# Hybrid streaming encoder on one core: norms ahead of the first products, block sums regrouped, first splits on GpSimd, scan steps ahead of weight steps

## The chip, the cores and the metric

The kernel runs on one core of a Trainium2 chip. The core has a matrix engine (TensorE, PE in the rows, with weight loads as PEld), a vector engine (VectorE, DVE), a scalar engine (ScalarE, ACT), GpSimd (POOL) and SyncE (SP), which here issues most DMA transfers. Each engine works through its own list of instructions in order; semaphores make one wait for another. SBUF is the on-chip memory of 128 partitions, PSUM the banks into which PE accumulates. The metric is the device time of one execution in microseconds (us); a kernel's time is the median of its runs. The profile comes from one more execution.

## The reference

One block over 1040 tokens (16 learned tokens and 1024 of the input), 1024 wide, all float32:

```
h = concat(meta_tokens, x)
u = rmsnorm(h) * norm_mix_g
proj = u @ w_in                     # mLSTM q,k,v,o,i,f and retention q,k,v,g: 4 + 4 heads
h_ml = sigmoid(o) * head_norm(mlstm_chunkwise(silu(conv4(q,k)), v, gates))
h_rt = silu(g) * head_norm(retention_chunkwise(rotary(q), rotary(k), v))
h = h + concat(h_ml, h_rt) @ w_out
a = causal_dwconv(rmsnorm(h) @ w_up)            # FF = 2816
h = h + (silu(a) * (rmsnorm(h) @ w_gate)) @ w_down
out = rmsnorm(h)[meta:]
```

Both chunked scans carry a state C from chunk to chunk: `num = scores @ v + q @ C`, then `C = decay * C + k^T v`. The head norm takes mean and variance of each token's 256 values.

## The kernel before

**Products.** Every large float32 product is made of three faster ones: each operand is split into hi (a rounded copy, made by ACT) and lo (the remainder, made by DVE), and hi·hi, hi·lo and lo·hi are accumulated in PSUM. On top of this most products are done in a scheme of seven block products instead of eight: the activations are cut into blocks 11, 12, 21, 22 (half of the tokens by half of the channels), and sums S1 to S4 of blocks (`usum`, split by `usplit`) are formed on DVE; the weights get such sums too.

**Opening.** The 1040 tokens come in five pieces (`RNG`). `first_norm(r)` squares a piece, adds the squares up, lets PE sum over partitions (pca), takes the square root and its reciprocal (rcola), has PE broadcast the result (pra), scales the piece in place (L652) and splits it into u11h/u11l and so on. Head 4 (the first of retention) is done in plain three-part form: `v4_group(c)` gives v and the gates of one chunk with the weights w0raw, split into w0hi/w0lo by `v0_split`, and `q4_group` gives q and k. Then come the block sums, and `o_steps(4)`, the first seven-block product (po4x, po4y), which uses S1 to S4 in its third to sixth product; `qk_steps(0)` (pq0x, pq0y) follows.

**Mixing heads.** From here the program deals steps out by a planner. `go(steps)` walks the products of a head's q/k, v and o weights; around each, `slot` runs one step (`tick`) of each pending generator (`pend`) and starts tasks from the list `side`: the scan steps of another head (`scan_a`: scores s, pt, kw; `scan_b`: u, n, C, the statistics bn), and what follows a scan. How many tasks start in a slot depends on an estimated load of DVE and ACT against PE (`load`, `RATE`, `watch`). Weight units are generators as well: `quartered` (splits and block sums of one weight), `m_unit`, `w_unit` (sums of w_out for later), `first_right`. They wait with `jwait` for raw weight tiles, of which there are four, and `m_unit` and `w_unit` also wait while `busy()` says that DVE or ACT is ahead of PE by more than 0.5. While this part is built, `pinned` keeps each engine's instructions in the order in which they were written; elsewhere a scheduler orders them.

**End of the mixer.** The product with w_out is the class `Seven` (object `mixw`), in stages 1, 65, 73, 4, 2 (pwx, pwy). Its first stage is dealt among the scan steps of head 7. In stages 65 and 73 DVE forms the right operands (wr, rr; `rsplit`, L1030), sums for later stages (`tsum`, L1098) and, at L1755, four sums for the last two tokens (acc<-wm,mm,acc), whose factors stand in the small table mm.

## Time and profile before

| | |
|---|---|
| median of 3 runs | 1598.24 us (1595.65 to 1604.74) |
| profiled execution | 1605.5 us, of which the span (first to last instruction) is 1603.7 us |
| mean granted PE clock | 0.974 of full speed |
| PE busy | 1511.2 us, 94% |
| DVE busy | 1112.6 us, 69% |
| ACT busy | 778.6 us, 49% |
| POOL busy | 67.5 us, 4% |

Rows of stretches read: start and end, length, then busy time and count for PE, PEld, DVE, ACT and POOL, the granted PE clock, the DMA share and GB/s. Rows of a timeline read: start, duration, engine, line, operation, output<-inputs, shape; in brackets the idle time of that engine just before, and what ended it. A row with xN at its end is N instructions in a row. Rows of waits read: who waited for what: us in total, times, the longest. The opening ends at about 118 us, where the first product of head 0 starts; the scans and weight products of the mixer go on to 800; the feed-forward part takes the rest.

### The profile page before, as it was taken

How to read it: one execution, taken by the hardware profiler on the slowest of the kernel's cores; microseconds unless marked ns; L12 is line 12 of the kernel's file. 1: busy time of each engine (PE TensorE's matmuls, PEld its weight loads, DVE VectorE, ACT ScalarE, POOL GpSimd, SP SyncE). 2: the span in 40 equal slices, each digit the busy share in tenths (PEclk: the TensorE clock that was granted, in tenths of full speed). 3: DMA queues.
4: the chain of work that ended last, by engine and by line, in shares of the span. 5: the costliest groups of instructions: out<-in, count | busy, mean ns of one | idle time of the engine just before them, and what ended most of it. 6: DMA issues, size and time to landing. Idle time of an engine off the chain costs nothing.

```text
span 1603.7 us, 25323 instructions
## 1 busy us (share of the span) xinstructions
PE 1511.2 (94%) x9799; PEld 1368.9 (85%) x9799; DVE 1112.6 (69%) x2161; ACT 778.6 (49%) x1506; POOL 67.5 (4%) x104
## 2 busy tenths in 40 slices
PE   5989998899899999899799999999999999999997
PEld 4878898799888989897588898999999999888887
DVE  6586666675686757683876678777766666677657
ACT  5244557574654355554345546544444444344444
POOL 0000000000000000000000000222220000000000
PEclk9899999999999999999899999999999999999999
DMA  6031235542654245659634225788874222943213
GB/s 221 27 106 55 73 119 172 164 121 78 152 180 155 80 119 170 185 173 371 219 104 132 86 82 182 206 204 205 210 188 113 79 79 81 372 164 112 92 53 106
DMA packets 107176, 232.17 MB, mean 145 GB/s; under 512 B 10808, under 2 KB 34048, under 8 KB 106880
## 3 DMA queue, kind: packets, MB, share of 16 engines
q1 hardware_dynamic: 96736, 201.12, 38.0%
q0 software_dynamic: 10176, 29.37, 9.6%
q8 instruction: 77, 1.26, 0.3%
q14 instruction: 43, 0.35, 0.1%
q10 hardware_dynamic: 144, 0.07, 0.0%
HBM read 179.10 MB, written 74.49 MB: 158 GB/s over the span
## 4 chain that ended last, share of the span: by engine, by line
PE 71%; DMA 12%; DVE 9%; issue 4%; ACT 4%; SPq 0%; POOL 0%; DVEq 0%; POOLq 0%; ACTq 0%
DMA accd<-raw_m 3%; PE pdx L671 3%; PE pdx L672 3%; PE pdx L673 3%; PE pup_x L672 2%; PE pup_x L673 2%; PE pga_x L672 2%; PE pup_x L671 2%; PE pga_x L673 2%; PE pga_x L671 2%; PE pdy L672 2%; PE pdy L671 2%; PE pdy L673 2%; PE pwx L672 2%; PE pwx L671 2%
## 5 line engine op out<-in xcount | busy, mean ns | idle before, releaser
L575 ACT CAST hi_up<-raw_up 128x512 fp32r<-128x512 f32 (+1 forms) x52 | 36.4, 719 | 106.0 <-PE pga_z L672 61.2
L671 PE MATMUL pup_x<-uh_g,hi_up 128*128 128x256 f32 (+1 forms) x240 | 67.1, 282 | 1.2 <-ACT uh_g L1612 1.2
L576 DVE TENSOR_TENSOR lo_ga<-fraw_ga,hi_ga 128x512 fp32r<-128x512 f32 (+1 forms) x52 | 41.9, 809 | 37.8 <-ACT hi_ga L575 37.6
L672 PE MATMUL pup_x<-ul_g,hi_up 128*128 128x256 f32 (+1 forms) x240 | 67.1, 281 | 0.1
L673 PE MATMUL pup_x<-uh_g,lo_up 128*128 128x256 f32 (+1 forms) x240 | 66.4, 282 | 0.0
L576 DVE TENSOR_TENSOR lo_up<-raw_up,hi_up 128x512 fp32r<-128x512 f32 (+1 forms) x52 | 41.3, 810 | 36.0 <-ACT hi_up L575 35.1
L576 DVE TENSOR_TENSOR lo_d<-rd,hi_d 128x1024 fp32r<-128x1024 f32 (+1 forms) x34 | 37.7, 1113 | 32.9 <-ACT hi_d L575 32.8
L575 ACT CAST hi_ga<-fraw_ga 128x512 fp32r<-128x512 f32 (+1 forms) x52 | 36.4, 719 | 45.6 <-PE pup_z L672 24.0
L672 PE MATMUL pdx<-ul_d,hi_d 128*128 128x512 f32 (+1 forms) x156 | 58.1, 375 | 0.0
L673 PE MATMUL pdx<-uh_d,lo_d 128*128 128x512 f32 (+1 forms) x156 | 57.6, 373 | 0.0
L575 ACT CAST hi_d<-rd 128x1024 fp32r<-128x1024 f32 (+1 forms) x34 | 32.3, 960 | 48.9 <-PE pdy L672 32.6
L672 PE MATMUL pdy<-ul_d,hi_d 128*128 128x512 f32 x132 | 51.9, 393 | 0.0
L673 PE MATMUL pdy<-uh_d,lo_d 128*128 128x512 f32 x132 | 51.3, 389 | 0.0
L671 PE MATMUL pdx<-uh_d,hi_d 128*128 128x512 f32 (+1 forms) x156 | 48.8, 374 | 0.0
L671 PE MATMUL pdy<-uh_d,hi_d 128*128 128x512 f32 x132 | 48.3, 392 | 0.0
L672 PE MATMUL pga_x<-ul_g,hi_ga 128*128 128x512 f32 x120 | 47.6, 397 | 0.0
L673 PE MATMUL pga_x<-uh_g,lo_ga 128*128 128x512 f32 x120 | 47.3, 394 | 0.0
L671 PEld LDWEIGHTS pup_x<-uh_g,hi_up 128*128 128x128 f32 x240 | 45.3, 189 | 2.3 <-ACT uh_g L1612 1.4
L671 PE MATMUL pga_x<-uh_g,hi_ga 128*128 128x512 f32 x120 | 47.1, 393 | 0.0
L1321 DVE BATCH_NORM_STATS2 bn<-n 128x6 f32<-128x256 f32 (+1 forms) x72 | 30.7, 426 | 23.5 <-ACT n L1317 8.8
L672 PEld LDWEIGHTS pup_x<-ul_g,hi_up 128*128 128x128 f32 x240 | 45.5, 189 | 1.1 <-DVE ul_g L1613 0.3
L673 PEld LDWEIGHTS pup_x<-uh_g,lo_up 128*128 128x128 f32 x240 | 44.6, 188 | 0.8
(1679 smaller groups left out, 5889.4 us busy)
## 6 DMA issues: line engine op xcount, KB each, us to landing
raw_up<-w_up_d SPq DMA_DIRECT2D x22, 512.0 KB, 4.4
fraw_ga<-w_gate_d SPq DMA_DIRECT2D x22, 512.0 KB, 4.5
acts<-cv SPq DMA_DIRECT2D x44, 256.0 KB, 4.3
wsd<-w_down_d POOLq DMA_DIRECT2D x44, 256.0 KB, 6.4
rd<-wsd SPq DMA_DIRECT2D x22, 512.0 KB, 3.5
raw_w<-w_out_d SPq DMA_DIRECT2D x20, 512.0 KB, 4.6
wsw<-raw_w SPq DMA_DIRECT2D x32, 256.0 KB, 2.3
raw_m<-w_out_d SPq DMA_DIRECT2D x14, 512.0 KB, 3.8
```

What stands on the lines that cost most here:

```text
L575: AC.copy(hi[:, o:o + n], x)
L576: V.tensor_tensor(lo[:, o:o + n], x, hi[:, o:o + n].bitcast(F32), ALU.subtract)
L671: m.append(PE.matmul(pt, ah, xh_, start=first and k == 0, stop=False, skip_group_check=True))
L672: PE.matmul(pt, ah, xl_, start=False, stop=False, skip_group_check=True)
L673: m.append(PE.matmul(pt, al, xh_, start=False, stop=last and k == n - 1, skip_group_check=True))
L1321: V.bn_stats(sb[:L], pn[:L, :DV])
```

## The change

- In `first_norm` the second square of the first two pieces is made by DVE rather than ACT; the last fold of the squares is left out, and PE sums two partial results instead (one more matmul per 128 tokens). The warm-up activation is Sqrt instead of Square.
- `w0lo` is subtracted on GpSimd. `v4_group` runs all hi·hi products, then lo·hi, then hi·w0lo.
- `first_norm(2)`, `(3)`, `(4)` are called earlier. The block sums S1 and S2 and their splits stand ahead of the v and q/k products of the second half of the tokens; S3 and S4 stand after these, in other buffers (S2 in r0/r1, S3 in r2/r3, S4 in uh2/ul2, with two copies on GpSimd that free x12).
- The generators of scan steps go into a list of their own, `front`, which `tick` steps ahead of the weight units in `pend`. The `busy()` waits are gone, the numbers in `RATE` for DVE and ACT are lower, a quarter of a weight waits only for the raw tiles that it needs, and the units for w_out's sums are dealt to other places.
- The statistics of a chunk (`bn_stats`) read ACT's copy in SBUF instead of the PSUM bank.
- At the end of the mixer, stage 1's products are dealt in quarters; the last tokens' sums (acc) and the sums of `tsum` are ordered behind the last `rsplit`; the former are written at steps 0 to 3 of stage 73 instead of 2 to 5, and their inputs are loaded in stage 65 into another buffer; the table mm lies in another pool.

```diff
@@ -85,7 +85,7 @@
-    RATE = {"PE": (0.004, 0.000445), "DVE": (0.15, 0.00105), "Activation": (0.2, 0.00083)}
+    RATE = {"PE": (0.004, 0.000445), "DVE": (0.12, 0.00098), "Activation": (0.1, 0.00083)}
@@ -139,7 +139,7 @@
-    mm = mxp.tile([P, 2 * 8, 2], F32, name="mm")
+    mm = per.tile([P, 2 * 8, 2], F32, name="mm")
@@ -175,7 +175,7 @@
-    AC.activation(warm[:, 0:1], epsc, AF.Square)
+    AC.activation(warm[:, 0:1], epsc, AF.Sqrt)
@@ -237,13 +237,14 @@
+    front = []
...
-    def spawn(g):
+    def spawn(g, q=pend):
...
-                pend.append(g)
+                q.append(g)
@@ -255,13 +256,14 @@
-        assert pend or evacs
+        assert pend or evacs or front
...
-        for g in list(pend):
-            if next(g, pend) is pend:
-                pend.remove(g)
+        for q in (front, pend):
+            for g in list(q):
+                if next(g, pend) is pend:
+                    q.remove(g)
@@ -359,7 +361,7 @@
-                yield from jwait(*js)
+                yield from jwait(*(js[x] for x in {0: (0,), 1: (1,), 2: (0, 2, 3)}.get(i, (0, 1, 2, 3))))
@@ -384,14 +386,14 @@
-        quartered((kind, h), (ja, jb), lambda: [jget(x)[:, i * HB:(i + 1) * HB] for x in (ja, jb) for i in (0, 1)], 1, {5: (jb,), 6: (ja,)}, nm)
+        quartered((kind, h), (ja, ja, jb, jb), lambda: [jraw[x][:, i * HB:(i + 1) * HB] if x in jraw else None for x in (ja, jb) for i in (0, 1)], 1, {5: (jb,), 6: (ja,)}, nm)
...
-        quartered(("vp", p), js, lambda: [jget(j) for j in js], 2, {3: (js[0],), 4: (js[2],), 5: (js[3],), 6: (js[1],)}, f"vp{p}")
+        quartered(("vp", p), js, lambda: [jraw.get(j) for j in js], 2, {3: (js[0],), 4: (js[2],), 5: (js[3],), 6: (js[1],)}, f"vp{p}")
@@ -405,14 +407,10 @@
-                    while busy():
-                        yield
...
-                    while busy():
-                        yield
@@ -432,13 +430,9 @@
-                while busy():
-                    yield
...
-                while busy():
-                    yield
@@ -538,11 +532,11 @@
-        u_fm("q", a, *w_units(p > 0))
+        u_fm("q", a)
...
-        u_fm("o", a, *v_units(p, 1), *m_units(prev), *w_units(p == 0))
-        u_fm("q", b, *(r_units(0, 1) if p == 2 else w_units(1)))
-        u_fm("o", b, *(v_units(p + 1, 0) if p < 2 else r_units(2, 3)), *m_units(a), *w_units(p < 2))
+        u_fm("o", a, *v_units(p, 1), *m_units(prev), *w_units(1))
+        u_fm("q", b, *(r_units(0, 1) if p == 2 else w_units(2)))
+        u_fm("o", b, *(v_units(p + 1, 0) if p < 2 else r_units(2, 3)), *m_units(a))
@@ -641,17 +635,20 @@
-        for x, y in zip(sq, xs):
-            AC.activation(x, y, AF.Square)
+        AC.activation(sq[0], xs[0], AF.Square)
+        if r < 2:
+            V.tensor_tensor(sq[1], xs[1], xs[1], ALU.mult)
+        else:
+            AC.activation(sq[1], xs[1], AF.Square)
...
-        V.tensor_tensor(sq[0][:, 0], sq[0][:, 0], sq[0][:, 1], ALU.add)
-        pr = rms(sq[0][:, 0], 0, n, f"a{r}", tmp.tile([P, 5], F32, tag="rcol", name=f"rcola{r}"), None, ptags=("tr", "upd"))
+        pr = rms(sq[0][:, 0], 0, n, f"a{r}", tmp.tile([P, 5], F32, tag="rcol", name=f"rcola{r}"), None, ptags=("tr", "upd"), more=[sq[0][:, 1]])
+        parts_ = [[u[:, :, j0:j1] for u in UB[f"{half + 1}{i + 1}"]] for i in range(2)]
...
-            h_, l_ = (u[:, :, j0:j1] for u in UB[f"{half + 1}{i + 1}"])
-            AC.copy(h_, x)
+            AC.copy(parts_[i][0], x)
+        for x, (h_, l_) in zip(xs, parts_):
@@ -676,7 +673,7 @@
-            V.tensor_tensor(w0lo[i], w0raw[i], w0hi[i].bitcast(F32), ALU.subtract)
+            G.tensor_tensor(w0lo[i], w0raw[i], w0hi[i].bitcast(F32), ALU.subtract)
@@ -702,15 +699,16 @@
-        for kb in range(KB):
-            u = UB[f"{half + 1}{kb // 4 + 1}"]
-            o = kb % 4 * nv
-            mm3(pv[:, :nv], tuple(x[:, kb % 4, j0:j0 + L] for x in u), tuple(x[kb // 4][:, o:o + nv] for x in (w0hi, w0lo)), kb == 0, kb == KB - 1)
+        for i, j in ((0, 0), (1, 0), (0, 1)):
+            for kb in range(KB):
+                u = UB[f"{half + 1}{kb // 4 + 1}"][i]
+                o = kb % 4 * nv
+                PE.matmul(pv[:, :nv], u[:, kb % 4, j0:j0 + L], (w0hi, w0lo)[j][kb // 4][:, o:o + nv], start=i + j + kb == 0, stop=j == 1 and kb == KB - 1, skip_group_check=True)
...
-        w = need(("q4", i))
+        w = need(("q4", i), 1 - i)
@@ -1318,7 +1316,7 @@
-        V.bn_stats(sb[:L], pn[:L, :DV])
+        V.bn_stats(sb[:L], num[slot][:L])
@@ -1408,7 +1406,7 @@
-            spawn(g)
+            spawn(g, front)
@@ -1460,19 +1458,15 @@
+    first_norm(2)
...
-    first_norm(2)
+    first_norm(3)
...
+    first_norm(4)
...
-    first_norm(3)
-    for c in (5, 6):
-        v4_group(c, next(ring0))
-    for i in range(2):
-        q4_group(i, 1, 16, 272, next(ring0))
-    first_norm(4)
@@ -1493,18 +1487,28 @@
+    need(("o", 4, 1), 0)
+    usum(0, "22", "21", "S1")
+    usum(0, "11", "21", "21")
+    usum(1, "S1", "11", "11")
+    usplit("S2", "11", "r0", "r1")
+    usum(1, "11", "12", "12")
+    usplit("S1", "S1", "uh3", "ul3")
+    for c in (5, 6):
+        v4_group(c, next(ring0))
+    for i in range(2):
+        q4_group(i, 1, 16, 272, next(ring0))
...
-    usum(0, "22", "21", "S1")
-    usum(0, "11", "21", "21")
-    usplit("S3", "21", "r0", "r1")
-    usum(1, "S1", "11", "11")
-    usum(1, "11", "12", "12")
-    usplit("S4", "12", "r2", "r3")
-    usplit("S2", "11", "uh2", "ul2")
-    usplit("S1", "S1", "uh3", "ul3")
+    usplit("S3", "21", "r2", "r3")
+    x12 = [st.tile([P, 2 * SB], F32, tag=f"A{i + 1}", name=f"s4_{i}").rearrange("p (k j) -> p k j", k=2) for i in range(2)]
+    for i in range(2):
+        G.tensor_copy(x12[i], part("12", i))
+    s1[:] = x12
+    need(("o", 4, 1))
+    usplit("S4", "S1", "uh2", "ul2")
@@ -1590,8 +1594,8 @@
-        for js in ((0, 1), (2, 3)):
-            slot(lambda: mixw.mms(t, js=js), pe=2)
+        for j in range(4):
+            slot(lambda: mixw.mms(t, js=(j,)))
@@ -1741,22 +1745,22 @@
-        if st == "73" and k == 0:
-            x = fp.tile([P, 4 * XW], F32, name="wm", tag="xh2", bufs=1)
+        if st == "65" and k == 5:
+            x = fp.tile([P, 4 * XW], F32, name="wm", tag="xl6", bufs=1)
...
-        if st == "73" and 2 <= k < 6:
-            i, j = divmod(k - 2, 2)
+        if st == "73" and k < 4:
+            i, j = divmod(k, 2)
...
-                V.scalar_tensor_tensor(y, x[:, b * D + j * HB:b * D + (j + 1) * HB], mm[:, 14 + b, i:i + 1], y, ALU.mult, ALU.add)
+                after(V.scalar_tensor_tensor(y, x[:, b * D + j * HB:b * D + (j + 1) * HB], mm[:, 14 + b, i:i + 1], y, ALU.mult, ALU.add), last["rsplit"][1])
...
-            mixw.tsum(3, k - 2)
+            after(mixw.tsum(3, k - 2), last["rsplit"][1])
...
-            mixw.tsum(3, KW - 2 + k)
+            after(mixw.tsum(3, KW - 2 + k), last["rsplit"][1])
...
```

First place, DVE in the opening. pra2, pra3 and pra4 are the broadcasts for norms 2 to 4, vz and pvm belong to the learned tokens, gts holds the gates. Before:

```order
L652 SCALAR_TENSOR_TENSOR x21_122<-x21_122,vec_72,pra3_573 128x272 x4
L652 SCALAR_TENSOR_TENSOR x22_125<-x22_125,vec_72,pra3_573 128x272 x4
L686 TENSOR_TENSOR vz_114<-pvm0_0_946,vz_114 16x256
L655 TENSOR_TENSOR u21l_133<-x21_122,u21h_132 128x4x272
L686 TENSOR_TENSOR vz_114<-pvm0_0_946,vz_114 16x256
L655 TENSOR_TENSOR u22l_131<-x22_125,u22h_130 128x4x272
L710 COPY gts_118<-pv4_3_453 128x2x4
L710 COPY gts_118<-pv4_4_480 128x2x4
L710 COPY gts_118<-pv4_5_589 128x2x4
L710 COPY gts_118<-pv4_6_616 128x2x4
L652 SCALAR_TENSOR_TENSOR x21_122<-x21_122,vec_72,pra4_706 128x256 x4
L652 SCALAR_TENSOR_TENSOR x22_125<-x22_125,vec_72,pra4_706 128x256 x4
```

Now:

```order
L708 COPY gts_118<-pv4_3_475 128x2x4
L649 SCALAR_TENSOR_TENSOR x21_122<-x21_122,vec_72,pra3_459 128x272 x4
L649 SCALAR_TENSOR_TENSOR x22_125<-x22_125,vec_72,pra3_459 128x272 x4
L652 TENSOR_TENSOR u21l_133<-x21_122,u21h_132 128x4x272
L708 COPY gts_118<-pv4_4_502 128x2x4
L621 RECIPROCAL rcola4_533<-rcola4_533 128x2
L652 TENSOR_TENSOR u22l_131<-x22_125,u22h_130 128x4x272
L649 SCALAR_TENSOR_TENSOR x21_122<-x21_122,vec_72,pra4_541 128x256 x4
L649 SCALAR_TENSOR_TENSOR x22_125<-x22_125,vec_72,pra4_541 128x256 x4
L1481 TENSOR_TENSOR s1_0_608<-x22_125,x21_122 128x1056
```

Between the scaling of norm 3 and of norm 4 stood the copies of the gates of four chunks (gts<-pv4_3 to pv4_6), each of which follows that chunk's products on PE, and three additions of the learned tokens; now one copy and the reciprocal stand there. On PE the same shows at the products: norm 2's broadcast stood at the end of the products of q/k's first piece. Before (pq4 is q/k of head 4, pv4 its v, pca the sum over partitions):

```order
L662 MATMUL pq4100_401<-u12l_129,hi_q4_1_0_224 128x272
L663 MATMUL pq4100_401<-u12h_128,lo_q4_1_0_225 128x272
L661 MATMUL pq4100_401<-u12h_128,hi_q4_1_0_224 128x272
L662 MATMUL pq4100_401<-u12l_129,hi_q4_1_0_224 128x272
L663 MATMUL pq4100_401<-u12h_128,lo_q4_1_0_225 128x272
L661 MATMUL pq4100_401<-u12h_128,hi_q4_1_0_224 128x272
L662 MATMUL pq4100_401<-u12l_129,hi_q4_1_0_224 128x272
L663 MATMUL pq4100_401<-u12h_128,lo_q4_1_0_225 128x272
L632 MATMUL pra2_438<-cs_73,rcola2_432 128x128 x2
L620 MATMUL pca3_565<-cs_73,sqr0_134 16x1
```

Now:

```order
L706 MATMUL pv4_1_272<-w0lo0_111,u11h_126 128x264 x4
L706 MATMUL pv4_1_272<-w0lo1_112,u12h_128 128x264 x4
L626 MATMUL pra1_323<-cs_73,rcola1_317 128x128
L614 MATMUL pca2_369<-cs_73,sqr0_134 128x1 x4
L706 MATMUL pv4_2_337<-w0hiq_109,u11h_126 128x264 x4
L658 MATMUL pq4000_391<-u11h_126,hi_q4_0_0_216 128x272
L658 MATMUL pq4100_417<-u11h_126,hi_q4_1_0_224 128x272
L626 MATMUL pra2_376<-cs_73,rcola2_368 128x128 x2
L706 MATMUL pv4_2_337<-w0hik_110,u12h_128 128x264 x4
```

pra2 has moved from row 106 of PE's list to row 19.

Second place, PE at the end of head 7's scan (u, n and s are scan steps, tr the transposes after it, v the transposes of v; pwx is stage 1 of the product with w_out). Before:

```order
L1302 MATMUL u7_6_8193<-n7_1_7880,kw7_6_8171 128x256
L1304 MATMUL n7_6_8195<-n7_1_7880,pt7_6_8161 128x256
L1306 MATMUL n7_6_8195<-C7_5_8174,qT7_7612 128x256
L1359 MATMUL tr7_0_0_8267<-cs_73,vz_114 128x16
L1359 MATMUL tr7_0_0_8267<-cs_73,n7_0_7879 128x128 x3
L1255 MATMUL s7_8_8225<-qT7_7612,kT7_7613 128x128
L1302 MATMUL u7_7_8229<-n7_1_7880,kw7_7_8207 128x256
L1359 MATMUL tr7_0_1_8284<-cs_73,vz_114 128x16
L1359 MATMUL tr7_0_1_8284<-cs_73,n7_0_7879 128x128 x3
L1304 MATMUL n7_7_8231<-n7_1_7880,pt7_7_8191 128x256
```

Now:

```order
L1300 MATMUL u7_7_8199<-n7_1_7771,kw7_7_8159 128x256
L1253 MATMUL s7_8_8184<-qT7_7587,kT7_7588 128x128
L1302 MATMUL n7_7_8201<-n7_1_7771,pt7_7_8156 128x256
L1304 MATMUL n7_7_8201<-C7_6_8171,qT7_7587 128x256
L668 MATMUL pwx2_8162<-wone2_7843,hi_w1_2_8187 128x512
L1357 MATMUL tr7_0_0_8231<-cs_73,vz_114 128x16
L1357 MATMUL tr7_0_0_8231<-cs_73,n7_0_7770 128x128 x3
L669 MATMUL pwx2_8162<-wone2_7843,hi_w1_2_8187 128x512
L670 MATMUL pwx2_8162<-wone2_7843,lo_w1_2_8188 128x512
L668 MATMUL pwx3_8177<-wone2_7843,hi_w1_2_8187 128x512
L669 MATMUL pwx3_8177<-wone2_7843,hi_w1_2_8187 128x512
L670 MATMUL pwx3_8177<-wone2_7843,lo_w1_2_8188 128x512
```

28 rows of scan steps stood together without a product between; now products of pwx stand between them.

Third place, DVE in stage 65 (L1755 and L1759 are the last tokens' sums, L1098 and L1096 `tsum`, L1030 and L1028 the low halves of rr and wr). Before:

```order
L1030 TENSOR_TENSOR wr65_21_8468<-wa0_8359,wr65_21_8468 128x512
L1755 SCALAR_TENSOR_TENSOR acc10_8739<-wm_8733,mm_115,acc10_8739 128x512
L1098 TENSOR_TENSOR wa2_8369<-wa4_8352,wa2_8369 128x512 x2
L1755 SCALAR_TENSOR_TENSOR acc11_8741<-wm_8733,mm_115,acc11_8741 128x512
L576 TENSOR_TENSOR lo_w65_2_8473<-raw_w65_2_8202,hi_w65_2_8472 128x1024
L1126 SCALAR_TENSOR_TENSOR wa0_8359<-wa0_8359,wa4_8352 128x512
L1098 TENSOR_TENSOR wa3_8374<-wa5_8314,wa3_8374 128x512
L576 TENSOR_TENSOR lo_w65_3_8510<-raw_w65_3_8293,hi_w65_3_8509 128x1024
L1098 TENSOR_TENSOR wa3_8374<-wa5_8314,wa3_8374 128x512 x3
L1030 TENSOR_TENSOR rr1_8342<-wa0_8359,rr1_8342 128x512
L1030 TENSOR_TENSOR wr65_20_8476<-wa0_8359,wr65_20_8476 128x512
```

Now:

```order
L570 TENSOR_TENSOR lo_w65_2_8482<-raw_w65_2_8297,hi_w65_2_8481 128x1024
L1028 TENSOR_TENSOR wr65_21_8477<-wa0_8368,wr65_21_8477 128x512
L1124 SCALAR_TENSOR_TENSOR wa0_8368<-wa0_8368,wa4_8361 128x512
L1028 TENSOR_TENSOR rr1_8351<-wa0_8368,rr1_8351 128x512
L1124 SCALAR_TENSOR_TENSOR wa0_8368<-wa0_8368,wa4_8361 128x512
L570 TENSOR_TENSOR lo_w65_3_8519<-raw_w65_3_8329,hi_w65_3_8518 128x1024
L1028 TENSOR_TENSOR wr65_20_8485<-wa0_8368,wr65_20_8485 128x512
L1096 TENSOR_TENSOR wa2_8378<-wa4_8361,wa2_8378 128x512
L1127 SCALAR_TENSOR_TENSOR wa0_8368<-wa0_8368,wa6_8388 128x512
L570 TENSOR_TENSOR lo_w65_4_8556<-wd0_8419,hi_w65_4_8555 128x1024
L1028 TENSOR_TENSOR rr0_8350<-wa0_8368,rr0_8350 128x512
```

The last tokens' sums are no longer here (they stand 40 rows further down), and one sum of `tsum` stands where there were five.

More of the change, by code (lines that the diff above doesn't have):

```diff
@@ L272, in flush @@
         rush[0] = True
-        while pend or evacs:
+        while pend or evacs or front:
             tick()
@@ L1418, in slot @@
         load["slot"] = load["PE"]
-        if pend or evacs:
+        if pend or evacs or front:
             tick()
@@ L1436, in drain @@
         while len(side) > keep:
-            assert able() or pend or evacs
+            assert able() or pend or evacs or front
             if able():
                 one()
-            if pend or evacs:
+            if pend or evacs or front:
                 tick()
```

## The prediction

> **What bounds the kernel now.** I read the page's busy line and chain first, then a table of stretches for where TensorE (PE) stands idle, then its list of waits, then the timeline at the long ones.
>
> ```profile
> PE 1511.2 (94%) x9799; PEld 1368.9 (85%) x9799; DVE 1112.6 (69%) x2161; ACT 778.6 (49%) x1506; POOL 67.5 (4%) x104
> PE 71%; DMA 12%; DVE 9%; issue 4%; ACT 4%; SPq 0%; POOL 0%; DVEq 0%; POOLq 0%; ACTq 0%
> ```
>
> PE works 94% of the span and carries 71% of the chain: whatever doesn't fill a hole of PE, or slow it, changes nothing. The holes lie like this (columns: busy us of PE, PEld, DVE, ACT, POOL, then PE's granted clock):
>
> ```profile
> 0.00:118.00 118.00, 88.45 (x614) 83.12 (x614) 81.31 (x160) 52.18 (x85) 0.31 (x5) 0.90 0.37 120
> 118.00:160.00 42.00, 38.50 (x287) 36.10 (x288) 28.89 (x66) 19.45 (x42) 0.21 (x2) 0.96 0.18 52
> 160.00:750.00 590.00, 553.02 (x4096) 520.31 (x4095) 400.98 (x928) 319.81 (x671) 11.31 (x18) 0.97 0.49 149
> 750.00:800.00 50.00, 37.16 (x158) 28.63 (x157) 37.02 (x72) 19.58 (x37) 0.00 (x0) 0.90 0.73 270
> 800.00:1590.00 790.00, 788.67 (x4607) 695.73 (x4607) 558.00 (x921) 366.26 (x669) 54.23 (x77) 1.00 0.49 142
> ...
> 27.40:34.20 6.80, 6.05 (x25) 5.65 (x26) 6.70 (x15) 1.83 (x3) 0.00 (x0) 0.50 0.01 2
> 34.30:41.10 6.80, 6.80 (x57) 6.80 (x55) 0.29 (x2) 0.95 (x3) 0.00 (x0) 1.00 0.00 0
> ```
>
> Idle PE time is 29.6 us in the first 118, 3.5 in the next 42, 37.0 in the scan stretch 160 to 750, 12.8 in 750 to 800, and only 1.3 in the 790 us after that. The last two rows show a second price: behind a hole of 3.1 us at 24 us, PE ran 25 products in 6.8 us at half clock, where the next 6.8 us took 57. Busy time times the missing clock gives what that costs: 88.45 x 0.10 = 8.8 us in the first stretch, 38.50 x 0.04 = 1.5, 553 x 0.03 = 16.6, 37.2 x 0.10 = 3.7. So a hole of some 3 us costs itself and about half of the 3.4 to 6.8 us behind it. [...]
>
> **The opening (0 to 160).**
>
> ```profile
> 8.37 1.28 ACT L624 ACT_TABLE_LOAD   x1
> 8.38 1.26 DVE L679 TENSOR_TENSOR w0lo<-w0raw,w0hiq 128x1056 fp32r<-128x1056 f32 x1 [1.12 <-ACT w0hiq L678]
> 9.66 0.25 ACT L624 ACTIVATE rcola<-pca,epsc 16x1 f32<-16x1 f32 x1
> 12.83 2.28 DVE L652 SCALAR_TENSOR_TENSOR x<-x,vec,pra 128x144 f32<-128x144 f32 x8
> 14.77 0.59 PE L661 MATMUL pv<-w0hiq,u11h 128*128 128x264 f32 x1 [3.29 <-ACT u11h L654]
> 27.44 0.59 PE L661 MATMUL pv<-w0hiq,u11h 128*128 128x264 f32 x1 [3.10 <-ACT u11h L654]
> ...
> 41.36 3.22 DVE L652 SCALAR_TENSOR_TENSOR x<-x,vec,pra 128x256 f32<-128x256 f32 x8 [4.66 <-PE pra L632]
> ...
> 72.19 3.22 DVE L652 SCALAR_TENSOR_TENSOR x<-x,vec,pra 128x256 f32<-128x256 f32 x8 [5.54 <-PE pra L632]
> 75.33 1.25 DVE L1487 TENSOR_TENSOR s<-x,x 128x1056 f32<-128x1056 f32 x1
> ...
> 98.07 0.39 PE L671 MATMUL po4x<-uS2h,hi_o 128*128 128x256 f32 x1 [3.75 <-ACT sig L736]
> 118.01 0.39 PE L671 MATMUL pq0y<-u12h,hi_q 128*128 128x264 f32 x1 [0.46 <-ACT sig L736]
> 129.27 0.39 PE L671 MATMUL pq0x<-uS2h,hi_q 128*128 128x264 f32 x1 [3.49 <-ACT rawq L736]
> ```
>
> The scaling of the last norm starts at 72.19, after DVE had waited 5.54 us for a two-matmul broadcast (pra) that stands on PE behind some 190 products. Only then do the block sums begin (75.33), and from there DVE is the late one: PE waits at 98 and 129. The changed order puts the matmuls of norms 2, 3 and 4 ahead of those products.
>
> I walked DVE's changed order with durations from the rows above and their like. First product: the sqrt table is no longer loaded at 8.37 (1.28 us), one square goes to DVE while ACT does the other, a fold goes, and the 1.26 us w0lo no longer stands between the folds and the scaling. That moves 14.77 to about 12.2. Norm 1's scaling still has some 11 us of DVE work ahead of it, so PE's second hole stays, at about 5 us with its two small neighbours. Then 7 us of DVE rows lead to norm 2's scaling (near 31, not 41.4), another 7 to norm 3's, 6 to norm 4's (near 43 to 47, not 72.2), and 13 operations of 1.25 us carry the first sums and splits to about 64, before PE is through with the head-4 products. PE: it was busy 88.45 - 8.8 = 79.6 us at full clock before 118, of which 1 us lies ahead of the first product. 12.2 + 78.6 + 5 (second hole) + 3.4 (half clock behind the start and the hole) + 2 for small waits = 101. So 118.0 moves to 101: 17 us. The ten added pca matmuls (0.2 us each) are in the 2.
>
> Is DVE there in time? It had worked 81.3 us up to 118; less two w0lo and folds (4 us) and with its 5.7 us of initial waiting that is about 83 to 90 us. So the sums no longer hold PE, and the wait at 129 loses perhaps a third (1 us). Sum: **18 us**, from 4 (DVE full from the start, so only the first-product gain and one sum wait are left) to 25 (the wait at 129 and its half clock go too).
>
> What is queued differently: on SP the rotary table for slot A now stands ahead of raw_q0a, and waits for the last block-sum split, so that load is held to about 79; it needs 5 us more and is wanted at 101. The two copies of x12 on POOL stand between the S1 split and the S4 split; S4 is wanted by the fifth of seven products of o4, some 10 us behind the first sum.
>
> **First splits on POOL.** The nearest row is a smaller POOL operation:
>
> ```profile
> 1597.26 1.41 POOL L2089 TENSOR_TENSOR resid<-resid,Rc 128x256 f32<-128x256 f32 x2 [382.13 <-ACT Rc L636]
> ```
>
> 0.72 us each for 256 columns, so an estimate of 3.0 us for 1056. From w0hi's end near 8.4 the pair ends at about 14.5. PE first needs it after 16 hi products, at about 17.5: hidden by 3 us. The low end is 0; the high end, were POOL twice as slow, is 3 us of waiting. I take 0. [...] No row here shows POOL's first arithmetic at a time when anything waited for it.
>
> **The end of the mixer (750 to 800).**
>
> ```profile
> 766.36 0.33 PE L1359 MATMUL tr<-cs,n 128*128 128x128 f32 x1 [1.80 <-ACT n L1350]
> 787.90 1.19 PE L671 MATMUL pwy<-rr,hi_w 128*128 128x512 f32 x4 [1.42 <-ACT rr L1030]
> 789.09 0.75 DVE L1755 SCALAR_TENSOR_TENSOR acc<-wm,mm,acc 128x512 f32<-128x512 f32 x1
> 793.23 1.89 DVE L1098 TENSOR_TENSOR wa<-wa,wa 128x512 f32<-128x512 f32 x3
> 795.04 0.68 DVE L1030 TENSOR_TENSOR rr<-wa,rr 128x512 fp32r<-128x512 f32 x1
> 795.78 0.79 PE L672 MATMUL pwy<-rr,hi_w 128*128 128x512 f32 x1 [6.69 <-DVE rr L1030]
> ```
>
> PE's longest hole but the first, 6.69 us, waits for rr's low half, which stands on DVE behind three of the sums of L1098 (0.63 us each) and after the last tokens' operations of L1755 (0.75). After the change L1755 stands a stage later and each sum behind the splits of its own step: 8 x 0.75 = 6 us leave the queue. They land in the next stage, where DVE is busy 558 of 790 us. Holes 1.42 and 6.69 and half of the 6.8 us behind them: 9.5 us, of which I leave 2. The scan's own tail (4.5 us of holes) gets stage products between its steps, since scan steps are now issued one slot at a time among them; I take 3.5 of 4.5. **11 us**, from 5 to 16.
>
> **The scan stretch (160 to 750).**
>
> ```profile
> PE n L1304 <- DVE bn L1321: 7.6, 5, 3.2
> PE u L1302 <- DVE C L1315: 7.2, 2, 4.2
> PE n L1304 <- DVE z L1336: 6.3, 3, 3.9
> PE tr L1359 <- ACT n L1350: 2.0, 2, 1.8
> ```
>
> The statistics now read ACT's copy in SBUF, so the PSUM bank that the next step's n needs is free once ACT has copied it. That can end the 7.6 us. The other two groups are DVE standing in line behind something else late; the order alone doesn't mend these, and the new order can bring others: scan steps go ahead of weight steps, the pacing waits in the weight units are gone. The list supports a gain of up to 7.6 + 2.0 and half as much clock, 14; a loss as large as the gain isn't excluded. I take **7**, from -12 to 16. Eight table loads fewer and five DVE operations fewer are worth nothing alone: ACT has half its time free.
>
> **After 800** nothing changes and PE has no hole: 0.
>
> **Sum.** 18 + 11 + 7 = 36 us. The profiled execution took 1605.5 us (span 1603.7), 7.3 above the median 1598.2; taken off the median: 1562.
>
> **Rivals.** (a) *DVE is the bound of the opening.* Between 75 and 110 it is nearly always busy; if its work fills the time all the way, the earlier norms only move the wait from 72 to the q0 products: 6 in the opening, 8 at the mixer's end, 2 between: 1582. Against it: 81 us of work in 118. (b) *All holes close*: 25 + 15 + 16: 1542. For it, the holes are one queue's tail in most cases; against it, several end on transfers. (c) *Not what it says*: PE's waits move to the next split and nothing is won beyond the first product, 5 us: 1593. (d) *Slower*: scan steps first. A step's n needs pt, C and the copy of the step before it (0.35, 0.48 and 0.37 us of work by their rows, more with the queues). With steps issued earlier and fewer products between, each of the 72 chunk steps may wait. At 0.4 us a step the 29 us from the other two places are eaten; at 0.7 us the time is 1569 + 72 x 0.7 = 1620. Against it: waits for C and pt now total 8 us, and the changed order puts the n products at least as far apart where they were closest.
>
> ```profile
> L1315 DVE SCALAR_TENSOR_TENSOR C<-C,dec,u x28: 449/478/485, 215.8 to 515.6; 128x257 f32<-128x257 f32 x28
> ```
>
> **How the numbers follow.** My forecast 0.45 (own range 1550 to 1576), (a) 0.20, (b) 0.10, (c) 0.10, (d) 0.15. About 8 us (0.5%) is what a measurement can tell from no change, so 1590 to 1606 is "same": (c) and a little of (a). Faster 0.74, same 0.11, slower 0.15. The range leaves out (d) and half of (b): 1540 to 1600.
>
> **What would show it.** In the profile after: first v4 product near 12.2; norm 4's scaling before 50; first pq0 product near 101; no hole over 2 us at rr; the n<-bn group gone from PE's waits; POOL's first operation near 3 us with PE not waiting for it. I am wrong if PE waits for w0lo, if DVE is full from 20 to 110 with PE still waiting at o4, or if new waits n<-C or n<-pt appear tens of times.

## The result, and the profile after

The changed kernel takes 1556.4 us (median of four runs, 1550.1 to 1560.1) against 1599.9 us before in the same sitting: a ratio of 0.9723, 95% interval 0.9676 to 0.9771. Forecast were 1562 us, 1540 to 1600. Its profiled execution has a span of 1557.9 us, 45.8 less than the profiled one before.

The page's busy line and chain, in the form shown before:

```profile
PE 1500.4 (96%) x9819; PEld 1362.4 (87%) x9819; DVE 1109.4 (71%) x2156; ACT 765.6 (49%) x1496; POOL 75.9 (5%) x108
PE 77%; DMA 9%; DVE 7%; issue 4%; ACT 2%; SPq 0%; POOL 0%; DVEq 0%; POOLq 0%; ACTq 0%
```

The large products are the same (PE's list has 20 small matmuls more); PE's busy time fell by 11 us, since less of it passed at half clock (the mean granted clock went from 0.974 to 0.980), and its share rose to 96%. To place the gain, both traces are cut at the same products: the first of head 0's q (pq0y), the first of the last head's o (po7x), and the matmul that sums the squares of the next norm over partitions (pcb). The fourth row of each table is the same length of time behind that matmul, for comparison. The stretches before:

```profile
0.00:118.00 118.00, 88.45 (x614) 83.12 (x614) 81.31 (x160) 52.18 (x85) 0.31 (x5) 0.90 0.37 120
118.00:708.70 590.70, 552.08 (x4120) 520.91 (x4121) 411.57 (x954) 319.55 (x675) 9.75 (x18) 0.97 0.44 130
708.70:906.10 197.40, 182.70 (x887) 150.59 (x885) 131.71 (x230) 89.93 (x161) 1.78 (x2) 0.96 0.57 194
906.10:1594.00 687.90, 686.43 (x4171) 613.02 (x4170) 485.34 (x813) 315.92 (x584) 54.23 (x77) 1.00 0.51 147
```

and in the changed kernel:

```profile
0.00:100.60 100.60, 83.13 (x634) 78.37 (x634) 78.62 (x154) 48.45 (x81) 8.99 (x9) 0.95 0.39 131
100.60:672.00 571.40, 547.00 (x4121) 517.54 (x4122) 413.24 (x955) 310.42 (x669) 9.70 (x18) 0.98 0.45 136
672.00:860.10 188.10, 182.17 (x886) 151.84 (x884) 129.75 (x230) 89.75 (x160) 1.75 (x2) 0.95 0.60 204
860.10:1548.00 687.90, 686.08 (x4171) 612.94 (x4170) 485.18 (x813) 316.05 (x585) 54.09 (x77) 1.00 0.50 148
```

The opening is 17.4 us shorter, the scans 19.3, the mixer's end 9.3. What follows, which the change doesn't touch, does the same 4171 matmuls in the same 687.9 us; up to the end of the span it takes 697.6 us before and 697.8 now. The second column shows how the stretches got shorter: PE stood idle for 29.6 us of the opening before and 17.5 after, 38.6 and 24.4 in the scans, 14.7 and 5.9 at the mixer's end. The rest of the gain in the opening and the scans is busy time that fell, at a better clock (0.95 for 0.90, 0.98 for 0.97).

Rows picked from the timeline of the changed kernel, at the places that the prediction names (the first broadcast, POOL's first operation, the scaling of the pieces, the first products):

```profile
8.46 2.42 POOL L676 TENSOR_TENSOR w0lo<-w0raw,w0hiq 128x1056 fp32r<-128x1056 f32 x1 [7.62 <-ACT w0hiq L675]
8.95 1.33 PE L626 MATMUL pra<-cs,rcola 16*128 16x16 f32 x4 [0.53 <-DVE rcola L619]
10.50 0.93 DVE L640 TENSOR_TENSOR sqr<-x 128x512 f32<-128x512 f32 x1 [1.45 <-DMA x<-h_in_d]
10.83 2.88 POOL L676 TENSOR_TENSOR w0lo<-w0raw,w0hik 128x1056 fp32r<-128x1056 f32 x1
11.35 2.28 DVE L649 SCALAR_TENSOR_TENSOR x<-x,vec,pra 128x144 f32<-128x144 f32 x8
13.55 1.25 PE L706 MATMUL pv<-w0hiq,u11h 128*128 128x264 f32 x4 [3.27 <-ACT u11h L650]
...
31.31 3.21 DVE L649 SCALAR_TENSOR_TENSOR x<-x,vec,pra 128x256 f32<-128x256 f32 x8
45.72 3.36 DVE L649 SCALAR_TENSOR_TENSOR x<-x,vec,pra 128x272 f32<-128x272 f32 x8 [0.39 <-PE pra L626]
53.64 3.22 DVE L649 SCALAR_TENSOR_TENSOR x<-x,vec,pra 128x256 f32<-128x256 f32 x8 [1.64 <-PE pra L626]
...
100.63 0.39 PE L668 MATMUL pq0y<-u12h,hi_q 128*128 128x264 f32 x1 [0.50 <-ACT sig L734]
110.31 0.39 PE L668 MATMUL pq0x<-uS2h,hi_q 128*128 128x264 f32 x1 [2.12 <-ACT rawq L734]
```

And the longest waits of PE from the scans on, with u<-C for comparison (rows between them left out):

```profile
PE pq3x L668 <- ACT hi_o L294: 3.8, 1, 3.8
PE s L1253 <- DVE pt L1277: 2.8, 2, 2.4
PE n L1302 <- ACT den L1317: 2.3, 3, 1.1
PE s L1253 <- ACT kT L909: 2.3, 1, 2.3
...
PE v L840 <- ACT n L1261: 2.0, 1, 2.0
PE tr L1357 <- DVE mx L1365: 1.9, 2, 1.6
PE pq6x L668 <- ACT hi_o L294: 1.9, 1, 1.9
PE tr L1357 <- DVE wa L1365: 1.6, 1, 1.6
...
PE u L1300 <- DVE C L1313: 0.4, 1, 0.4
```

n<-bn (7.6 us before), n<-z (6.3), u<-C (7.2) and pwy<-rr (8.1) are gone or nearly so. Others have come in their place, though smaller: s<-pt was 0.8 before and is 3.8 in two rows now (2.8 and 1.0).

### The profile page after: what moved, and what is told of

Read it like the earlier page. It is cut to its first block, busy times and chain, and to the rows that moved or that the text cites. A ratio compares the mean times of both kernels' runs of the same rounds, so it can differ in the third digit from the quotient of the medians.

```text
span 1557.9 us, 25386 instructions
## 1 busy us (share of the span) xinstructions
PE 1500.4 (96%) x9819; PEld 1362.4 (87%) x9819; DVE 1109.4 (71%) x2156; ACT 765.6 (49%) x1496; POOL 75.9 (5%) x108
## 3 DMA queue, kind: packets, MB, share of 16 engines
q1 hardware_dynamic: 96736, 201.12, 38.6%
## 4 chain that ended last, share of the span: by engine, by line
PE 77%; DMA 9%; DVE 7%; issue 4%; ACT 2%; SPq 0%; POOL 0%; DVEq 0%; POOLq 0%; ACTq 0%
PE pdx L668 3%; PE pdx L670 3%; PE pdx L669 3%; PE pup_x L669 2%; PE pup_x L670 2%; PE pga_x L669 2%; PE pup_x L668 2%; PE pga_x L670 2%; PE pga_x L668 2%; DMA raw_w<-w_out_d 2%; PE pdy L668 2%; PE pdy L670 2%; PE pwx L668 2%; PE pdy L669 2%; PE pwx L670 2%
## 5 line engine op out<-in xcount | busy, mean ns | idle before, releaser
L570 DVE TENSOR_TENSOR lo_d<-rd,hi_d 128x1024 fp32r<-128x1024 f32 (+1 forms) x34 | 37.7, 1113 | 32.9 <-ACT hi_d L569 32.7
L1253 PE MATMUL s<-qT,kT 128*128 128x128 f32 (+1 forms) x144 | 28.3, 278 | 6.2 <-DVE pt L1277 2.8
```

Source lines behind the costliest of these rows:

```text
L570: V.tensor_tensor(lo[:, o:o + n], x, hi[:, o:o + n].bitcast(F32), ALU.subtract)
L1253: PE.matmul(s[:, :L], k, q, start=True, stop=True)
```

## The experiments

The theory to test was the prediction's: three places that do not touch one another, each with its cause (the order of the norms; the statistics' PSUM reads; the queue ahead of rr). The rivals: the places are coupled, or each gain has another cause. All numbers against before are ratios with 95% intervals; the stretches are those of one profiled execution each, cut as above.

| kernel | ratio to before | opening | scans | mixer's end |
|---|---|---|---|---|
| before | 1 | 118.0 | 590.7 | 197.4 |
| changed | 0.9723 (0.9676 to 0.9771) | 100.6 | 571.4 | 188.1 |
| opening alone | 0.9860 (0.9842 to 0.9878) | 99.9 | 583.4 | 196.7 |
| scan part alone | 0.9859 (0.9831 to 0.9887) | 117.9 | 559.8 | 192.3 |
| mixer's end alone | 0.9927 (0.9904 to 0.9950) | 115.6 | 586.8 | 188.0 |
| changed, statistics from PSUM | 0.9678 (0.9660 to 0.9695) | 99.1 | 568.7 | 184.1 |
| changed, one list | 0.9691 (0.9665 to 0.9717) | 98.9 | 564.8 | 186.8 |
| changed, pacing waits back | 0.9864 (0.9833 to 0.9895) | 99.6 | 587.9 | 190.1 |
| changed, old rates | 0.9720 (0.9686 to 0.9754) | 99.6 | 577.4 | 189.2 |
| changed, old units | 0.9760 (0.9729 to 0.9791) | 98.9 | 576.9 | 188.9 |
| changed, statistics from PSUM and one list | 0.9669 (0.9652 to 0.9686) | 99.3 | 567.4 | 179.4 |
| changed, old order of the opening | 0.9735 (0.9717 to 0.9754) | 102.1 | 569.6 | 188.8 |
| changed, old sums at the end | 0.9711 (0.9695 to 0.9726) | 99.3 | 570.0 | 186.9 |
| before without pacing waits | 0.9961 (0.9949 to 0.9973) | 116.9 | 582.7 | 193.1 |

Stretches that a kernel doesn't edit show how far one profile can be trusted. The old opening reads 118.0, 117.9, 115.6 and 116.9 us, the new one, with the calls in the new order, 98.9 to 100.6. The old scans behind the old opening read 590.7 and 586.8. So differences of 2 us in the opening and 4 us in the scans say nothing.

### The three places, each alone

The kernel before with the opening's hunks of the diff (warm-up, `first_norm`, `v0_split`, `v4_group`, `q4_group`, the calls and the block sums):

> Before, with the opening's edits alone (norms ahead, block sums regrouped, w0lo on POOL, Sqrt as the warm-up, squares and fold). Theory that the three places are independent: the first product of head 0 starts at about 101 us as in the changed kernel (118 before), and the time falls by 17 to 20 us, to about 1581. Rival, that the places are coupled (the lead of the opening also shifts the scans against their transfers and empties some of the scan stretch's holes): it falls by 25 us or more, to 1575 or less; or it is given back in the scan stretch and falls by less than 10.

with those of the scans (`RATE`, `front`, `quartered`, `m_unit`, `w_unit`, the dealing of units, `bn_stats`):

> Before, with the scan part's edits alone (front list, load rates, no pacing waits, waits by quarter, units dealt otherwise, statistics from the SBUF copy). Independent places: the opening stays at 118 us, the stretch from there to the first pwx product is some 16 us shorter, total 12 to 18 us less, about 1585. Coupled: less than 8 us.

and with those of the mixer's end (the table mm, the quarters of stage 1, the last tokens' and later stages' sums):

> Before, with the edits at the mixer's end alone (products dealt in quarters, the last tokens' sums and the sums for later stages behind the splits, table in another pool). Independent places: PE's wait for rr falls from 6.7 us to under 1, total 9 to 12 us less, about 1588. Coupled, that is, if the tail gained from the scan steps' own list: 4 us or less, with the holes in the transposes still there.

The medians are 1579.0, 1578.0 and 1589.5 us against 1601.8 for before in that sitting: 22.8, 23.8 and 12.3 us. So each place gains by itself, and none of them needs another. But they are no sum. The product of the three ratios is 0.965, the three together have 0.9723: about 12 us are lost in the combination, with 2 to 22 possible by the intervals of all four ratios. The table says where to look: the scan edits alone shorten the scans by 31 us, the opening's edits alone by 7 (of which 4 may be chance), all together by 19. The scans with the scan edits alone:

```profile
117.90:677.70 559.80, 538.09 (x4121) 509.78 (x4122) 410.78 (x954) 309.21 (x668) 9.70 (x18) 0.99 0.46 137
```

PE idles 21.7 us here and 24.4 in the changed kernel, nearly the same; but busy time is 538.1 against 547.0 for the same 4121 matmuls, at clock 0.99 against 0.98. So of the 11.6 us between these two stretches 8.9, three quarters, are half-clock time. About half of the 11.6 us may be the choice of executions, for the profiled one of the changed kernel is its slowest (1560.1 us, 3.7 above the median) and that of the scan edits their fastest (1575.3, 2.7 below). Two holes of the changed kernel carry most of the half-clock time, 3.8 us up to 397.4 (pq3x) and 2.29 us up to 438.7 (s<-kT), each with a long stretch at clock 0.50 (6.8 and 10.2 us) that sets in within the hole or up to 1.7 us behind it:

```profile
438.69 0.40 PE L1253 MATMUL s<-qT,kT 128*128 128x16 f32 x2 [2.29 <-ACT kT L909]
...
396.00:402.80 6.80, 5.37 (x24) 5.37 (x25) 4.92 (x17) 5.93 (x12) 0.00 (x0) 0.50 0.58 203
440.40:450.60 10.20, 10.20 (x42) 8.15 (x41) 8.47 (x18) 4.16 (x10) 0.94 (x2) 0.50 0.27 40
```

The first expectation's threshold for independence (17 to 20 us) was passed by 3 us, and the rival's 25 was not reached. The scans of that kernel are 7 us shorter than before, but an unedited scan stretch varies by 4, so whether the earlier opening also spares waits later stays open.

### Statistics from the PSUM bank again

```diff
-        V.bn_stats(sb[:L], num[slot][:L])
+        V.bn_stats(sb[:L], pn[:L, :DV])
```

> The changed kernel with the statistics read from the PSUM bank again. If these reads were what held the bank in the scan stretch: 6 to 14 us slower than the changed kernel (1562 to 1570), and PE's waits n<-bn come back with 5 us or more. If the scan steps' own list and the lifted pacing did it: within 3 us of the changed kernel's 1556, n<-bn under 2 us.

1550.4 us: not slower, if anything faster by half a per cent (the intervals of the two ratios overlap a little). PE's wait on the statistics does come back:

```profile
PE n L1302 <- DVE bn L1319: 4.0, 3, 2.7
```

but it costs nothing in the total. The reads of the PSUM bank were a wait, not the cause of the gain.

### Scan steps in the common list

```diff
-            spawn(g, front)
+            spawn(g)
```

> The changed kernel with scan steps put into the common list again, behind the weight steps that are already there. If the list of their own is what shortens the scan stretch (559.8 us from the first product of head 0 to the last head's o products with the scan edits alone, 590.7 before): 8 to 15 us slower than the changed kernel's 1556, stretch 580 or more. If it is the pacing, the rates or the units: within 4 us.

1551.1 us, not slower either. The list of their own, of which the change's name tells, brings nothing in this kernel.

### Pacing waits back, old rates, old units

```diff
+                    while busy():
+                        yield
                     t = st.tile([P, HB], F32, tag="mt", name=f"mt{k}_{j}")
...
+                while busy():
+                    yield
                 V.tensor_tensor(v22, v22, v21, ALU.add)
```

> The changed kernel with the pacing waits of the units for w_out put back. If they held raw tiles, and so the loads and splits behind them, too long: 5 to 12 us slower, with waits of the q, k products for hi splits (pq<-hi) of 3 us or more again in several places. If they did not matter: within 3 us.

> The changed kernel with the old load estimates for DVE and ACT, so that fewer scan steps start in a slot. If the denser dealing matters: 5 to 12 us slower and steps left to be run in a heap at the heads' ends (forced), with holes at v and tr. If not: within 3 us.

(`RATE` as before in that kernel, and in the next one `jwait(*js)` for all tiles and the old places of `w_units`.)

> The changed kernel with the old waits for all tiles of a weight and the old places of the units for w_out's sums. If earlier splits of a quarter matter: 5 to 12 us slower, with the waits of pq, po for hi splits larger than the 5.7 us (pq3x, pq6x) of the changed kernel. If not: within 3 us.

The pacing waits are the one part of the scan edits whose return costs much: 1578.9 us, 22 us above the changed kernel, more than was expected. The scans take 587.9 us, nearly the 590.7 of before. PE's waits for hi splits of weights, 5.7 us in the changed kernel, are now 18; 11.3 of them lie in the scans (pq, po), and 6.7 in the mixer's end (pwx, at 750 us):

```profile
PE pwx L676 <- ACT hi_w L577: 6.7, 1, 6.7
PE pq3x L676 <- ACT hi_o L294: 3.9, 1, 3.9
PE po1x L676 <- ACT hi_o L294: 3.0, 1, 3.0
PE po3x L676 <- ACT hi_o L294: 2.5, 1, 2.5
PE pq6x L676 <- ACT hi_o L294: 1.9, 1, 1.9
```

That fits a picture in which a unit that waits for its turn keeps two of the four raw tiles, so that the next weight arrives late. The picture isn't shown, though. From the issue of a w_out load to the issue of its stores the tiles were held 12.3 us on average with the waits and 10.1 without (16.2 and 15.3 for the loads of `m_unit`), differences of 1 to 2 us. The old rates cost nothing (1557.5 us), the old units 6 us (1562.4, though the intervals overlap).

By an estimate, the waits cost more here than all scan edits together bring. By the first experiments the opening and the mixer's end without any scan edit would have 0.9860 x 0.9927 = 0.979, if the two are independent. This kernel, with all scan edits but the lifted waits, has 0.9864, some 12 us more (5 to 19 by the intervals). So the other scan edits seem to lose time as long as the waits stand.

### Before, without the pacing waits

The same four lines of `busy()` taken out of the kernel before.

> The kernel before with nothing changed but the pacing waits of the units for w_out left out. If these waits are enough of a cause by themselves: 12 to 23 us faster than before, and most of it between 160 and 700 us. If they matter only with the denser dealing: within 5 us of before.

1595.7 us, 5 us faster (0.9961, 0.9949 to 0.9973), less than a quarter of what they are worth in the changed kernel. Its scans still have the waits n<-bn and n<-z, which the changed kernel doesn't have, and a longer wait for pt than either (0.8 us before, 3.8 in the changed kernel):

```profile
PE n L1296 <- DVE bn L1313: 7.7, 8, 4.1
PE s L1247 <- DVE pt L1271: 5.3, 3, 2.7
PE n L1296 <- DVE z L1328: 4.8, 2, 4.5
```

So lifting the waits is needed for the gain and isn't enough for it: it takes their removal together with something else of the scan edits. Since the statistics, the list and the rates can each be taken back at no cost, and the units at 6 us, no single partner carries it; which combination does was not tried, so the cause of the scans' gain stays open beyond that.

### The old order of the opening

`first_norm(2)` to `(4)` called late again, block sums behind all products of head 4, in the old buffers; the short chain, the POOL splits and the three passes of `v4_group` stay.

> The changed kernel with the opening's old order of calls (norms 2 to 4 late, block sums behind all head-4 products, S2 to S4 in the old buffers), but with the short chain to the first product and w0lo on POOL. If the order of the norms makes the opening: first product of head 0 back to 115 to 117 us, 14 to 20 us slower than the changed kernel's 1556. If the short chain and the freed DVE make it: under 108 us, 8 us slower at most.

The first product of head 0 comes at 102.08 us instead of 100.63 (98.9 to 99.9 in the eight other kernels with the new order), and the total is 1558.6 us, 2 us more than the changed kernel and inside its interval. So the order of the calls brings at most some 3 us of the opening's 17, and the rest comes from what stayed. The scaling of norms 2 to 4 in this run:

```profile
31.01 3.20 DVE L649 SCALAR_TENSOR_TENSOR x<-x,vec,pra 128x256 f32<-128x256 f32 x8
54.12 3.36 DVE L649 SCALAR_TENSOR_TENSOR x<-x,vec,pra 128x272 f32<-128x272 f32 x8 [0.50 <-PE pra L626]
60.35 3.22 DVE L649 SCALAR_TENSOR_TENSOR x<-x,vec,pra 128x256 f32<-128x256 f32 x8
```

Norm 2 stands where it stands in the changed kernel (31.3), and norm 4 at 60 rather than 54; before it was 72.2. The opening isn't laid out as it is written: a scheduler orders it. How many matmuls PE's list has up to norm 2's and norm 4's broadcast, for the kernel before with single edits (read from the compiled order, not timed):

```
                                    pra2   pra4
before                               113    323
w0lo on GpSimd alone                 116    323
v4 in three passes alone             113    323
shorter sum of squares alone          50    243
changed, old order of calls           52    247
changed                               52    212
```

These are single matmuls. A row of the list holds up to four matmuls of one kind, and with three passes more of them fall into one row, so that row numbers shrink though nothing moves. The shorter sum of squares (a square on DVE, a fold left out) is what moves the broadcasts; the calls bring norm 4's forward by another 35 matmuls. How much of the time each of these parts is worth was not measured.

### The old sums at the mixer's end

The last tokens' sums and those of `tsum` back in their old places, the table mm and the quarters as changed.

> The changed kernel with the last tokens' sums and the sums for later stages placed as before, stage 1's products still in quarters. If the queue ahead of rr's low half is the cause: PE's wait for rr returns with 4 to 7 us and the half clock behind it, 8 to 12 us slower. If the quarters and the new dealing carry the mixer's end: within 3 us.

1554.5 us, no slower than the changed kernel. The sums of L1755 (L1759 here) are again on DVE between 746 and 755, in stage 65, and yet PE doesn't wait for rr, because the first of rr's splits is now ahead of them:

```profile
730.71 0.68 DVE L1028 TENSOR_TENSOR rr<-wa,rr 128x512 fp32r<-128x512 f32 x1
...
746.11 0.74 DVE L1759 SCALAR_TENSOR_TENSOR acc<-wm,mm,acc 128x512 f32<-128x512 f32 x1
```

What is left of the edits there is the pool of the small table mm and the quarters. The compiled order tells them apart (not timed): with mm moved to the pool `per` and nothing else, rr's first low half goes from row 1148 of DVE's list to row 1121, ahead of the first of the last tokens' sums (1133); with the quarters alone it stays behind all eight. And in the kernel of this run, whose sums stand in their old places, mm put back into mxp sends rr from row 1113 to row 1147, behind all eight sums. The pool mxp, in which mm lay, is closed at that place, and the pool that holds rr is opened in its stead; as long as the last reader of mm is one of the eight sums, rr comes after them. The four profiled kernels with mm in mxp (before, opening alone, scan part alone, no pacing) all wait for rr, by 2.8 us (no pacing) to 8.1 (before); here the second and third of them,

```profile
PE pwy L675 <- DVE rr L1034: 5.1, 1, 5.1
...
PE pwy L665 <- ACT rr L1024: 3.9, 1, 3.9
PE pwy L666 <- DVE rr L1024: 3.2, 1, 3.2
```

and none of those with mm in `per` does. So the compiled order names the pool as what holds rr back, but the pool alone was not timed: what it is worth by itself stays open between 0 and the 12 us of the mixer's end alone.

### Both costless parts left out

Statistics from the PSUM bank and one list, in one kernel.

> The changed kernel with two of its parts left out together: statistics from the PSUM bank, and scan steps in the common list (each alone measured about 6 us below the changed kernel). If each part has a cost of its own: 1542 to 1548. If both only shift steps against the half-clock stretches, so that the gains are no sum: 1549 to 1558.

1547.2 us (1545.2 to 1551.1), ratio 0.9669, 95% interval 0.9652 to 0.9686: the fastest median of the study. Its interval still overlaps a little with that of the changed kernel, and more with those of the kernels that leave out one of the two parts, so it can't be told from these. The scans are 4 us shorter than in the changed kernel and the mixer's end 8.7:

```profile
99.30:666.70 567.40, 544.63 (x4120) 513.63 (x4121) 413.28 (x955) 309.36 (x668) 9.69 (x18) 0.98 0.45 138
666.70:846.10 179.40, 174.81 (x887) 146.27 (x886) 129.01 (x231) 89.88 (x161) 1.77 (x2) 1.00 0.63 213
```

At the mixer's end 887 matmuls take 174.8 us at clock 1.00 where the changed kernel's 886 take 182.2 at 0.95: 7.4 of the 8.7 us are clock, not waiting. That holds for the whole kernel: the granted clock, averaged over the span, is 0.983 in the four runs of the changed kernel and 0.988 in the five of this one. An estimate from that, 0.005 of 1550 us, is 8 us, nearly all of the 9 us between the medians. So it isn't shown that the two parts cost anything by work of their own.

## Why the prediction was right, and where it was not

- **The size.** Forecast 36 us, measured 43.5 (medians), 45.8 (profiled). The likeliest case held and its own range (1550 to 1576) too. By places: opening 18 forecast, 17.4 found; mixer's end 11 and 9.3; scans 7 and 19.3, which is beyond the upper end of 16 given for it. So two places came out in size, and the third was far too small; its gain hangs on an edit to which the forecast gave nothing. That the total came out is in part luck.
- **Opening, first product.** Forecast 12.2, found 13.55. The table load ahead of the sqrt (1.28 us) is gone, but DVE's scaling started at 11.35, only 1.5 us earlier than before, where the forecast needs 2.6. PE's broadcast was done at 10.3; the square of the next piece, which the change gives to DVE, stood ahead of the scaling and had waited for its load until 10.50. Norm 1's hole was 2.4 + 1.2 + 1.8 = 5.4 us (forecast 5).
- **Opening, norms and sums.** Norm 2's scaling at 31.3 (near 31), norm 4's at 53.6 (43 to 47 was too early; its broadcast still waited 1.64 us on PE), the sums and the first two splits done at 75 instead of 64. The first q0 product at 100.6 against 101: the first product was 1.4 us late, PE's work with its half clock took 80.6 us instead of 82.0, and the small waits took 1.1 instead of 2, so the close hit is partly luck. The step that fails is the cause, "the changed order puts the matmuls of norms 2, 3 and 4 ahead of those products": the order of the calls is worth 2 us in the total (not clear of noise), and by the compiled order most of the same move comes from the shorter sum of squares, through the scheduler. The forecast of the effect held because it was read from the compiled order, which has the move whatever made it.
- **POOL.** Estimated 3.0 us each and an end at 14.5; found 2.42 and 2.88, end 13.7, and PE needs the first result at 19.3. The first subtraction begins 0.08 us after w0hi ends, behind 7.62 us in which POOL had stood idle, and PE's list of waits has none for w0lo.
- **Mixer's end.** The wait for rr is gone as forecast. The step "L1755 stands a stage later and each sum behind the splits of its own step" is not its cause: with the sums back nothing is lost. The edit that was left out of the working, the table's pool, is what the compiled order points to. The other 3.5 us, from the scan's tail, hardly came: without the waits for rr, PE's holes in this stretch are 5.9 us, where 14.7 - 8.1 = 6.6 stood before.
- **Scans.** The step "the statistics now read ACT's copy ... That can end the 7.6 us" is right on the wait and wrong on the time: with the reads back in the PSUM bank the wait returns with 4.0 us and the total does not rise. The lifted pacing, which the prediction listed only as a danger, is the part whose return costs 22 us. Rival (d), scan steps first as a loss of 0.4 us or more a step, did not happen in the changed kernel: PE's waits for pt and C fell from 8 us to 4.2. With the pacing waits back, though, the waits for pt alone are 8.2 us, and the kernel is some 12 us slower than the estimate for one without any scan edit.
- **Rival (a)**, DVE as the bound of the opening, did not happen: DVE was busy 78.6 of 100.6 us and PE's holes from 30 to 100 us are 0.6 us.

## What to carry to other kernels

Where a scheduler lays out the program, argue from the compiled order and not from the order of the calls, and look at what holds an instruction back there, a small table in a pool that is about to close as well as a long queue. Gains of single parts that are read from single waits did not add up here (0.965 as a product, 0.9723 together): holes of 1.69, 2.29 and 3.80 us on PE came with 3.4, 10.2 and 6.8 us at clock 0.50, one of 2.12 us (at 110 us of the changed kernel) with none, and which holes remained changed with the edits. Single profiles of the same code differed as well, by up to 2.4 us in the opening and 3.9 in the scans, so a stretch is worth comparing only where it differs by more. A rule that paces background work by an estimate is worth a run without it, in the kernel that has everything else.

## What was not expected of the hardware

- Half-clock stretches were not all of one length: behind the 2.29 us hole at 439 PE ran 10.2 us at 0.50 while busy all the time (row above). In the fastest kernel a hole of 1.69 us at the same place was followed by only 3.4 us:

```profile
437.82 0.40 PE L1253 MATMUL s<-qT,kT 128*128 128x16 f32 x2 [1.69 <-ACT kT L909]
...
438.80:442.20 3.40, 3.40 (x18) 3.17 (x16) 3.16 (x7) 2.14 (x6) 0.00 (x0) 0.50 0.10 39
```

- The clock also halved with no hole in the trace. At 840 us of the changed kernel 32 products with a single column each (pe, for the last two tokens) follow one another; PE is busy throughout, and from 843.2, ahead of the last of them, 6.8 us run at clock 0.50. In the fastest kernel the same 32 products are followed by no half clock (third row):

```profile
840.00:843.20 3.20, 3.20 (x29) 3.11 (x28) 1.85 (x3) 0.99 (x2) 0.00 (x0) 0.99 0.00 0
843.20:850.00 6.80, 6.80 (x20) 5.63 (x20) 3.83 (x9) 4.38 (x9) 0.00 (x0) 0.50 0.66 248
...
832.80:839.60 6.80, 6.80 (x31) 5.51 (x32) 5.12 (x12) 5.52 (x11) 0.00 (x0) 1.00 0.82 309
```

PE counts as busy there in a trace whose ends of matmuls are modelled. In the kernel before, 3.4 us at half clock stand right behind the 32 products, which start from 887.4 to 890.8:

```profile
891.00:894.40 3.40, 3.40 (x9) 2.67 (x9) 2.08 (x7) 3.11 (x6) 0.00 (x0) 0.50 0.69 255
```

So part of the lead of the fastest kernel over the changed one at the mixer's end is that it has none.
